# Block copies and additions put out one by one by a count of the DMA queue, in a one-core hybrid layer

## The chip, the cores and the metric

The kernel runs on one core of a Trainium2 chip. The metric is the device time of one execution in microseconds, the median of several runs. All arrays are 32-bit floats; matrix products get near to that precision because each operand is split into a high and a low part and three products of the parts are added.

## The reference

One layer for 512 tokens of width 1024: two branches (a gated delta rule, then a rotary retention) read the same projection; their outputs are gated, mixed and added to the input; an MLP with squared ReLU follows.

```python
xn = rmsnorm(x, n_mix_pre)
proj = xn @ w_in                                  # 1024 x 14352
qa, ka, va, za, beta_logit, a_dt, qb, kb, vb, gb, gate_a, gate_b = _split_cols(proj, IN_SIZES)
...                                               # branch A: conv, silu, l2norm, 8 heads, chunks of 64
oa = chunk_gated_delta_rule(qa, ka, va, beta, g)
oa = rmsnorm(oa, norm_a) * jax.nn.silu(za)
ya = oa.reshape(b, s, A_V) @ w_br_a               # 2048 x 1024
...                                               # branch B: rotary, 4 heads of 256 / 512
ob = chunk_retention(qb, kb, vb)
ob = rmsnorm(ob, norm_b) * jax.nn.silu(gb)
yb = ob.reshape(b, s, B_V) @ w_br_b               # 2048 x 1024
mix = (jax.nn.sigmoid(gate_a) * ya + jax.nn.sigmoid(gate_b) * yb) @ w_out
x = x + rmsnorm(mix, n_mix_post)
hn = rmsnorm(x, n_mlp_pre)
ff = jnp.square(jax.nn.relu(hn @ w_up)) @ w_down  # 1024 x 4096 x 1024
return x + rmsnorm(ff, n_mlp_post)
```

## The kernel before

All weights are read from DRAM in blocks of 512 KB (128 x 4 x 256 or 128 x 2 x 512). `weights` (line 96) issues the load of a block into a `raw` tile on the queue of SyncE (SP). Then ScalarE (ACT) casts it to the high part `whi` (L119) and VectorE (DVE) subtracts to get the low part `wlo` (L120). The raw tiles come from pools of two buffers: `ring`, and from the end of head 0 of branch B on also `ych`, in turn.

There are three stages. *Phase A* (to about 490 us) makes branch A. Its products are issued in an order that a planner, the class `Clock`, writes from costs: `Clock.matmul` (L598), `Clock.transpose` (L607). Four gate chains (`g2` = 0 to 3) end it piece by piece; each makes `og` (an activation on ACT at L1228, a product on DVE at L1230) from what a transpose left, and the next transpose and products need it. *Branch B* goes through four heads h. At the change of a head come the products of the decayed scores with the values (L86 to L88, tiles `dl`), on ACT the squares `osq` of the result (L1419), and the loads of the next head's query and key weights. The products of value and gate projection of a head, and the two output gates ga and gb, go through `token_product` (L247). The *MLP* is last (after about 1000 us).

Nine column pairs of the weights, ga, vg0 to vg3, gb and three of `w_down` (dn0 to dn2), are multiplied by a scheme with seven block products in place of eight (`seven`). It needs four sums of weight blocks. The class `BlockSums` makes them in DRAM, by the DMA engines alone: each `copy` (L138, on SP's queue) copies 512 KB from the weights to a tile `sums`, and each addition (`add_blocks`, L166, on the queue of GpSimd, POOL) adds 512 KB to it, as a DMA that accumulates. An addition waits for its copy and for earlier additions that it reads. There are 9 x 8 = 72 copies and 72 additions. Later, `block_weights` (L153) loads the sums like weights.

How they are placed before the change: from the 14th load on, each call of `weights` is followed by one copy on SP's queue while the list `trickle` is longer than `later_copies` (32, after head 0 16, in the MLP 8 and 0). Additions go out in batches: 14, 14 and 12 at the gate chains g2 = 1, 2 and 3; 8 behind the load of `dec` in heads 2 and 3; 8 in each of two groups of the MLP. POOL's queue, which keeps the order, also carries these loads and stores of branch B: `rope` (the rotary table), `dec` (a head's decay, one buffer), `ya_d` (branch A's output put by in DRAM) and `ya` (the same fetched again).

`tc.issue_after` sets only where an instruction stands in the order of its queue; it makes nothing wait. `high_priority(ahead)` in `split_weights` puts a cast up to 200 places ahead in ACT's and DVE's order.

Of the kernel before, what the change touches and what calls it, by code (L numbers as in the profile page):

```python
# [10 lines left out]
F32 = mybir.dt.float32  # L11
F32R = mybir.dt.float32r
# [3 lines left out]
ALU = mybir.AluOpType  # L16
# [3 lines left out]
P = 128  # L20
T = 512
D = 1024
# [4 lines left out]
OFF_QB, OFF_KB, OFF_VB, OFF_GB = 6160, 7184, 8208, 10256  # L27
OFF_GA, OFF_GBR = 12304, 13328
SMALL_US, CONV_US, TOK_US, PK_US, INV_US, DB_US = 10.5, 6.5, 2.5, 2.0, 46, 1.2
VT_US, KS_US, PX_US, PC_US, GATE_US, FEAT_US, INV_PRIO, CONV_PRIO, SMALL_PRIO, KEY_PRIO, DECAY_US, AHEAD, TR_US, REC_PRIO, OUT_PRIO = 2.5, 2.4, 3.5, 2.4, 11.0, 1.0, 0, 600, 800, 600, 20.0, 700, 2.2, 900, 900  # L30
# [31 lines left out]
def hybrid_block_kernel(ctx: ExitStack, tc: tile.TileContext, a: dict, out: bass.AP):  # L62
    nc = tc.nc
    x_d = a["x"][0]
    w_in = a["w_in"][0]
    w_br = [a["w_br_a"][0], a["w_br_b"][0]]
# [4 lines left out]
    raw_pools = [(ring, "raw")]  # L71
    loads = itertools.count()
    trickle = []
    later_copies = [32]
    ahead = [200]
# [5 lines left out]
    dr = ctx.enter_context(tc.tile_pool(name="dr", bufs=2, space=DRAM))  # L81

    def mm3(ps, lhs, rhs, first, last):
        lh, ll = lhs
        rh, rl = rhs
        nc.tensor.matmul(ps, lh, rh, start=first, stop=False)  # L86
        nc.tensor.matmul(ps, lh, rl, start=False, stop=False)  # L87
        nc.tensor.matmul(ps, ll, rh, start=False, stop=last)  # L88
# [18 lines left out]
    def copy_block(load):  # L107
        sums, part, k = trickle.pop(0)
        with tc.issue_after(load.ins):
            sums.copy(part, k)  # L110

# [14 lines left out]
    class BlockSums:  # L126


        def __init__(self, src, c1, c2, tag):
            def block(kh, c):  # L130
                return src[4 * kh * P : 4 * (kh + 1) * P, c : c + 512].rearrange("(k p) c -> p k c", p=P)

            self.w12, self.first = block(0, c2), [block(0, c1), block(0, c1), block(1, c2), block(1, c1)]
            self.t = [dr.tile([P, 4, 512], F32, tag=f"{tag}{i}", name="sums", bufs=1) for i in range(4)]
            trickle.extend((self, i, k) for i in (2, 1, 3, 0) for k in (0, 2))

# [3 lines left out]
        def adds(self):  # L140

            for i, k in ((2, 0), (1, 0), (3, 0), (2, 2), (1, 2), (3, 2), (0, 0), (0, 2)):
                src = (self.w12, self.t[2], self.w12, self.t[1])[i]
                yield self.t[i][:, k : k + 2, :], src[:, k : k + 2, :]
# [15 lines left out]
    adds = itertools.chain.from_iterable(sums.adds() for sums in [ga_sums] + vg_sums + [gb_sums] + down_sums)  # L160

    def add_blocks(mark, n):

        with tc.issue_after(mark.ins):
            for dst, src in itertools.islice(adds, n):
                tc.keep_in_program_order(nc.gpsimd.dma_start(dst, src, accum_op=ALU.add))  # L166

# [66 lines left out]
    def token_product(quarters):  # L234

        pinned = []

        def product(pss, x, ks, wts, first):
            wh, wl = wts
            xh, xl = quarters[x]  # L240
            for t in range(2):
                tt = slice(t * P, (t + 1) * P)
                for kk in range(2):
                    k = 2 * ks + kk
                    lhs, rhs = (xh[:, k, tt], xl[:, k, tt]), (wh[:, kk, :], wl[:, kk, :])
                    for i in range(3):
                        m = nc.tensor.matmul(  # L247
                            pss[t], lhs[i // 2], rhs[i % 2],
                            start=first and k + i == 0, stop=k + i == 5, skip_group_check=not first,
                        )  # L250
# [415 lines left out]

    clock = Clock()

    def product_features(src, xs, c0, ncols, kts, krow0, finish):
# [176 lines left out]
    ya_marks = []  # L846
# [58 lines left out]
    with delta_rule:  # L905
# [297 lines left out]
        def gate_chain(g2):  # L1203
# [4 lines left out]
            for hh in range(2):  # L1208
                for t in range(4):
# [99 lines left out]
        )  # L1309
        prev = ogs[3]  # L1310
        ahead[0] = 200


    with tc.tile_pool(name="pb", bufs=1) as pb_:
        rope = pb_.tile([P, 2, T], F32, name="rope")
        nc.gpsimd.dma_start(rope, a["c_rope"])
        cos, sin = rope[:, 0, :], rope[:, 1, :]
# [37 lines left out]
        def scores(h, rows):  # L1355
            dec = pb_.tile([P, T], F32, tag="dec", name="dec")
            decay = nc.gpsimd.dma_start(dec, a["c_decay"][h])
# [8 lines left out]
            if h == 0:  # L1366
                ya_marks.append(ya_partial(3, prev))
            scs = []
            for i in range(4):
                t0 = min(i * P, 256)  # L1370
                n = T - t0
# [11 lines left out]
                nc.vector.tensor_tensor(sc[:, :n2], ps[:, n - n2 : n], dec[:, :n2], ALU.mult)  # L1383
                sh, sl = (pb_.tile([P, n2], F32R, tag=f"s{i}{j}", name="s") for j in range(2))
                nc.scalar.copy(sh, sc[:, :n2])
# [57 lines left out]
        for h in range(4):  # L1443
            scs, og = scores(h, rows)
            if h == 0:

                def gate_a(t, half, src):
# [37 lines left out]
        kept = []  # L1485
        for i in (1, 0, 3, 2):
            keep = None
            if i != 2:
                w = pf.tile([P, 2, D], F32R, tag=f"f{i}", name="keep")
                keep = w[:, 0, :], w[:, 1, :]  # L1490
            kept.append(weights(w_br[1], 12 + len(kept), 1, 0, D, keep))
        mix = [act.tile([P, 8, T], F32R, tag="actT", name="actT") for _ in range(2)]
# [24 lines left out]
    with tc.tile_pool(name="pm", bufs=1) as pm:  # L1517
# [112 lines left out]
        wpost = broadcast_row(a["norm_mlp_post"][0], "post")  # L1630
        later_copies[0] = 8

# [101 lines left out]
        for grp in range(4):  # L1734
            sq = Squares(grp)
            for half in range(2):
                for th in (None,) if grp or half else (1, 0):
                    tt = slice(0, T) if th is None else slice(256 * th, 256 * th + 256)
                    pss = feature_major(w_up, [h[:, :, tt] for h in hn], grp * 1024 + half * 512, 512, 8)
                    for f in range(4):  # L1740
                        with tc.high_priority(150 * half):
                            sq.take(half, f, pss[f], th)
                            if half and f % 2 and not sq.last:
                                sq.first_sums(f - 1)
            if grp < 2:
                later_copies[0] = 0
                add_blocks(sq.sums_mark, 8)
            if not sq.last:
# [51 lines left out]
```

## Time and profile before

| | |
|---|---|
| three runs | 1361.91, 1370.55, 1366.67 us; median 1366.67 |
| the profiled execution | 1371.82 us, span 1370.0 us |
| TensorE (PE) | 1338.1 us busy, 98% of the span |
| VectorE (DVE), ScalarE (ACT) | 885.6 us (65%), 634.0 us (46%) |
| GpSimd (POOL) | 97.3 us (7%), nearly all of it issuing DMAs |
| DMA queue q1 (SP's and ACT's transfers) | 185.10 MB, 42.6% of the 16 DMA engines' span |
| DMA queue q0 (POOL's transfers) | 49.45 MB, 20.7% |

The span runs from the first to the last instruction of one execution; the time is what the device reports for it, a little more. The busy share of an engine is a mean over stages; PE's idle time, about 24 us in 1370, lies in a few gaps. Percentages of the queues are the time of their packets against all 16 engines, so a share near 1 in a stretch means that the transfers there are limited by the engines.

### The profile page before, as it was taken

To read this page: it belongs to the slowest core of one execution; us is meant where nothing else is said; L and a number is where in the kernel's file an instruction comes from. 1 tells how busy PE (TensorE), PEld (TensorE's weight loads), DVE (VectorE), ACT (ScalarE), POOL (GpSimd) and SP (SyncE) were. 2 spreads that over 40 slices of the span, in tenths; PEclk is the share of its full clock that TensorE was granted. 3 is DMA by queue.
4 is the path that set the end of the run, shared out by engine and by line. 5 is a ranking of instruction groups with operands and counts; after the bars stand their busy time and mean duration, and the time that the engine had idled before them with its cause. 6 is when DMAs were issued, how large, how long until landed. Compare 5 with 4: busy or idle time off the path is not lost.

```text
span 1370.0 us, 17550 instructions
## 1 busy us (share of the span) xinstructions
PE 1338.1 (98%) x6639; PEld 1106.6 (81%) x6639; DVE 885.6 (65%) x1515; ACT 634.0 (46%) x1118; POOL 97.3 (7%) x110
## 2 busy tenths in 40 slices
PE   9999999989999999999989989999999999999997
PEld 7888888878878878788868878888789888888886
DVE  6889858474466356767457567578776744828535
ACT  5783336543333423553433343355355736436441
POOL 2101110012010000000100100000001111000000
PEclk9999999999999999999999999999999999999999
DMA  5349995799892234693893882465549899635421
GB/s 185 130 139 220 216 179 127 159 231 221 193 223 65 75 116 135 218 305 105 202 287 102 193 212 69 146 212 172 192 139 275 218 284 206 218 98 168 135 82 62
DMA packets 114437, 236.79 MB, mean 173 GB/s; under 512 B 7398, under 2 KB 31120, under 8 KB 113840
## 3 DMA queue, kind: packets, MB, share of 16 engines
q1 hardware_dynamic: 95792, 185.10, 42.6%
q0 software_dynamic: 17824, 49.45, 20.7%
q8 instruction: 52, 0.85, 0.3%
q10 hardware_dynamic: 736, 1.12, 0.2%
q14 instruction: 33, 0.27, 0.1%
HBM read 231.43 MB, written 79.71 MB: 227 GB/s over the span
## 4 chain that ended last, share of the span: by engine, by line
PE 80%; DMA 8%; DVE 6%; ACT 5%; issue 1%; ACTq 0%; DVEq 0%; POOLq 0%
PE mm L598 17%; PE mm L87 10%; PE mm L86 10%; PE mm L88 10%; PE mm L247 10%; PE dl L247 10%; PE dl L598 6%; DMA raw<-in_w_in_dram 5%; DVE wlo L120 2%; DMA raw<-sums 2%; ACT whi L119 1%; PE tr L607 1%; PE tr L327 1%; PE dl L86 1%; PE dl L87 1%
## 5 line engine op out<-in xcount | busy, mean ns | idle before, releaser
L120 DVE TENSOR_TENSOR wlo<-raw,whi 128x1024 fp32r<-128x1024 f32 x254 | 310.0, 1222 | 264.1 <-ACT whi L119 263.4
L119 ACT CAST whi<-raw 128x1024 fp32r<-128x1024 f32 x254 | 266.9, 1052 | 419.8 <-PE mm L87 92.5
L598 PE MATMUL mm<-actT,whi 128*128 128x512 f32 x448 | 146.3, 408 | 0.0
L247 PE MATMUL mm<-whi,xsum 128*128 128x512 f32 x384 | 121.5, 390 | 0.0
L88 PE MATMUL mm<-hn,wlo 128*128 128x512 f32 (+1 forms) x288 | 105.4, 366 | 0.0
L87 PE MATMUL mm<-hn,whi 128*128 128x512 f32 (+1 forms) x288 | 105.3, 366 | 0.0
L86 PE MATMUL mm<-hn,whi 128*128 128x512 f32 (+1 forms) x288 | 105.3, 366 | 0.0
L598 PEld LDWEIGHTS mm<-actT,whi 128*128 128x128 f32 x448 | 81.7, 191 | 15.5
L247 PE MATMUL dl<-whi,actT 128*128 128x512 f32 x288 | 92.2, 390 | 0.0
L598 PE MATMUL mm<-whi,actT 128*128 128x512 f32 x256 | 87.8, 406 | 1.1 <-DVE qf L827 1.0
L598 PE MATMUL mm<-actT,wlo 128*128 128x512 f32 x224 | 88.7, 396 | 0.0
L247 PEld LDWEIGHTS mm<-whi,xsum 128*128 128x128 f32 x384 | 71.9, 188 | 14.9
L247 PE MATMUL mm<-wlo,xsum 128*128 128x512 f32 x192 | 75.0, 391 | 0.1
L598 PE MATMUL mm<-whi,og 128*128 128x512 f32 x192 | 64.2, 402 | 0.0
L247 PEld LDWEIGHTS dl<-whi,actT 128*128 128x128 f32 x288 | 54.1, 188 | 11.1
L86 PEld LDWEIGHTS mm<-hn,whi 128*128 128x128 f32 x288 | 54.3, 189 | 8.8
L88 PEld LDWEIGHTS mm<-hn,wlo 128*128 128x128 f32 x288 | 54.3, 189 | 8.7
L87 PEld LDWEIGHTS mm<-hn,whi 128*128 128x128 f32 x288 | 54.3, 189 | 8.7
L247 PE MATMUL dl<-whi,ffq 128*128 128x512 f32 x192 | 61.0, 389 | 0.0
L166 POOL DMA_DIRECT2D sums<-sums x36 | 30.0, 833 | 387.0 <-DMA sums<-in_w_in_dram 189.7
L598 PEld LDWEIGHTS mm<-whi,actT 128*128 128x128 f32 x256 | 48.1, 188 | 11.4 <-issue 1.7
L247 PE MATMUL dl<-wlo,actT 128*128 128x512 f32 x144 | 56.3, 391 | 0.6 <-DVE wlo L120 0.6
(376 smaller groups left out, 2804.6 us busy)
## 6 DMA issues: line engine op xcount, KB each, us to landing
raw<-in_w_in_dram SPq DMA_DIRECT2D x97, 512.0 KB, 5.0
raw<-sums SPq DMA_DIRECT2D x72, 512.0 KB, 4.5
sums<-in_w_in_dram SPq DMA_DIRECT2D x48, 512.0 KB, 8.8
sums<-sums POOLq DMA_DIRECT2D x36, 512.0 KB, 8.1
raw<-in_w_up_dram SPq DMA_DIRECT2D x36, 512.0 KB, 4.9
raw<-in_w_down_dram SPq DMA_DIRECT2D x26, 512.0 KB, 4.6
sums<-in_w_in_dram POOLq DMA_DIRECT2D x24, 512.0 KB, 11.4
sums<-in_w_down_dram SPq DMA_DIRECT2D x24, 512.0 KB, 10.6
```

The costliest lines, as they stand in the source:

```text
L86: nc.tensor.matmul(ps, lh, rh, start=first, stop=False)
L87: nc.tensor.matmul(ps, lh, rl, start=False, stop=False)
L88: nc.tensor.matmul(ps, ll, rh, start=False, stop=last)
L119: nc.scalar.copy(hi[:, :n], raw[:, :n])
L120: nc.vector.tensor_tensor(lo[:, :n], raw[:, :n], hi[:, :n], ALU.subtract)
L166: tc.keep_in_program_order(nc.gpsimd.dma_start(dst, src, accum_op=ALU.add))
L247: m = nc.tensor.matmul(pss[t], lhs[i // 2], rhs[i % 2], start=first and k + i == 0, stop=k + i == 5, skip_group_check=not first,)
L327: nc.tensor.transpose(ps, src, ident)
L598: m = tc.keep_in_program_order(nc.tensor.matmul(*args, **kwargs))
L607: tc.keep_in_program_order(nc.tensor.transpose(ps, src, ident if by is None else by))
```

## The change

Line numbers move: after the change a weight load is L102, a copy L165, an addition L132, a load of sums L185, `rope` L1345, `dec` L1386, `ya_d` L1486 and `ya` L1501.

*The count.* A function `pace` is called behind every load, those of `block_weights` too. It keeps two times in us: `spent`, how far PE's work is (in phase A the planner's clock, then the sum over matmuls by `tick`), and `queued`, until when the DMA engines are taken by what was issued. Each load adds 2.0, each copy 2.0, each addition 3.4; while less than 6.0 us are queued, the next job goes out behind the load, a copy and an addition in turn. An addition is ready when all copies of its group have been put out. `queued` begins at 60. `BlockSums.weights` would put out what is missing of a group before its loads. Batches and `later_copies` are gone.

*The queue.* `rope`, `dec`, `ya_d` and `ya` are issued by ACT (`nc.scalar`). `dec` has two buffers.

*Space.* The second pool of raw tiles, `ych`, opens before the unit of gate ga, where it was after the end of head 0. The eight score tiles of a head lie in one tile `s` of 2560 columns, and the fourth kept block of `w_br_b` lies there too at the end of the stage, where it was in `ring`.

```diff
+JOBS_FROM, LOAD_US, COPY_US, ADD_US, BACKLOG = 60.0, 2.0, 2.0, 3.4, 6.0
...
+    trickle, later_adds = [], []
+    added, spent, queued, clocks = [False], [None], [JOBS_FROM], []
...
+    def tick(n):
+        if spent[0] is not None:
+            spent[0] += 0.0135 + n / 2400
...
-        if paced and i >= 13 and len(trickle) > later_copies[0]:
-            copy_block(load)
+        pace(load)
...
+    def pace(load):
+
+        if clocks:
+            spent[0] = clocks[0].now
+        if spent[0] is None:
+            return
+        queued[0] = max(queued[0], spent[0]) + LOAD_US
+        with tc.issue_after(load.ins):
+            while (trickle or later_adds) and queued[0] < spent[0] + BACKLOG:
+                ready = len(later_adds) > -(-len(trickle) // 8) * 8
+                if ready and (added[0] or not trickle):
+                    add_block()
+                    queued[0] += ADD_US
+                elif trickle:
+                    copy_block()
+                    queued[0] += COPY_US
+                added[0] = not added[0]
+
+    def add_block():
+        dst, src = later_adds.pop(0)
+        tc.keep_in_program_order(nc.gpsimd.dma_start(dst, src, accum_op=ALU.add))
...
         def weights(self, i, ks):
+            while any(job[0] is self for job in trickle):
+                copy_block()
+            while any(dst is t for dst, src in later_adds for t in self.parts):
+                add_block()
             return block_weights(self.t[i - 1][:, 2 * ks : 2 * ks + 2, :])
...
-        nc.sync.dma_start(raw.rearrange("p (k c) -> p k c", k=2), block)
+        load = nc.sync.dma_start(raw.rearrange("p (k c) -> p k c", k=2), block)
+        pace(load)
...
-            if g2:
-                add_blocks(ya_marks[-1], (0, 14, 14, 12)[g2])
...
+        spent[0] = clocks.pop().now
...
-        nc.gpsimd.dma_start(rope, a["c_rope"])
+        nc.scalar.dma_start(rope, a["c_rope"])
...
-            dec = pb_.tile([P, T], F32, tag="dec", name="dec")
-            decay = nc.gpsimd.dma_start(dec, a["c_decay"][h])
-            if h > 1:
-                add_blocks(decay, 8)
+            dec = pb_.tile([P, T], F32, tag="dec", name="dec", bufs=2)
+            nc.scalar.dma_start(dec, a["c_decay"][h])
...
+            sall = pb_.tile([P, 2560], F32R, tag="s", name="s")
...
+                raw_pools.append((pb_, "ych"))
                 gate_unit(ga_sums, OFF_GA, gate_a)
                 for t in range(4):
-                    nc.gpsimd.dma_start(ya_d[:, t, :], acc_t[:, t, :])
+                    nc.scalar.dma_start(ya_d[:, t, :], acc_t[:, t, :])
...
-            if h == 0:
-                raw_pools.append((pb_, "ych"))
-                later_copies[0] = 16
...
-            kept = nc.gpsimd.dma_start(ya[i], ya_d[:, 2 * i : 2 * i + 2, :])
+            kept = nc.scalar.dma_start(ya[i], ya_d[:, 2 * i : 2 * i + 2, :])
...
-            if grp < 2:
-                later_copies[0] = 0
-                add_blocks(sq.sums_mark, 8)
```

How this moves instructions, at three places. First the queue of SP early in phase A, at about 96 to 121 us of the profile before; `raw` are loads, `sums` copies. Before:

```order
L96 DMA raw<-in_w_in_dram 128x2x512
L138 DMA sums<-in_w_in_dram 128x2x512
L96 DMA raw<-in_w_in_dram 128x2x512
L138 DMA sums<-in_w_in_dram 128x2x512
L96 DMA raw<-in_w_in_dram 128x4x256
L138 DMA sums<-in_w_in_dram 128x2x512
```

and after the change, around the same loads:

```order
L102 DMA raw<-in_w_in_dram 128x2x512 x2
L165 DMA sums<-in_w_in_dram 128x2x512
L102 DMA raw<-in_w_in_dram 128x2x512
L165 DMA sums<-in_w_in_dram 128x2x512 x2
L102 DMA raw<-in_w_in_dram 128x2x512
L165 DMA sums<-in_w_in_dram 128x2x512 x2
L102 DMA raw<-in_w_in_dram 128x4x256
L165 DMA sums<-in_w_in_dram 128x2x512 x2
L102 DMA raw<-in_w_in_dram 128x4x256
L165 DMA sums<-in_w_in_dram 128x2x512 x2
```

Before, copies begin seven loads earlier and go one behind each load; now they begin later, nine of them behind five loads. In the rest of phase A there are about three copies to four loads; before, one to each up to the 56th load and none behind it.

Second, the queue of POOL from the end of phase A to head 3. Before:

```order
L166 DMA sums<-in_w_in_dram 128x2x512 x2
L1316 DMA rope<-in_c_rope_dram 128x1024
L1357 DMA dec<-in_c_decay_dram 128x512 x2
L1455 DMA ya_d<-acc 128x1024 x4
L1357 DMA dec<-in_c_decay_dram 128x512
L166 DMA sums<-in_w_in_dram 128x2x512
L166 DMA sums<-sums 128x1024 x2
L166 DMA sums<-in_w_in_dram 128x2x512
L166 DMA sums<-sums 128x1024 x2
L166 DMA sums<-in_w_in_dram 128x2x512 x2
L1357 DMA dec<-in_c_decay_dram 128x512
L166 DMA sums<-in_w_down_dram 128x2x512
```

and after the change:

```order
L132 DMA sums<-in_w_in_dram 128x2x512 x3
L132 DMA sums<-sums 128x1024 x2
L132 DMA sums<-in_w_in_dram 128x2x512
L132 DMA sums<-sums 128x1024 x2
L132 DMA sums<-in_w_in_dram 128x2x512 x2
L132 DMA sums<-in_w_down_dram 128x2x512
L132 DMA sums<-sums 128x1024 x2
L132 DMA sums<-in_w_down_dram 128x2x512
```

Nothing but additions is left there; no `dec` stands ahead of them.

Third, the queue of SP at the change from head 2 to head 3 (about 790 to 826 us before), loads of query and key weights and of `w_br_b`. Before there is no copy:

```order
L96 DMA raw<-in_w_in_dram 128x4x256 x4
L96 DMA raw<-in_w_br_b_dram 128x2x512 x4
```

and after the change:

```order
L102 DMA raw<-in_w_in_dram 128x4x256
L165 DMA sums<-in_w_down_dram 128x2x512
L102 DMA raw<-in_w_in_dram 128x4x256
L165 DMA sums<-in_w_down_dram 128x2x512
L102 DMA raw<-in_w_in_dram 128x4x256 x2
L165 DMA sums<-in_w_down_dram 128x2x512
L102 DMA raw<-in_w_br_b_dram 128x2x512
L165 DMA sums<-in_w_down_dram 128x2x512
L102 DMA raw<-in_w_br_b_dram 128x2x512
L165 DMA sums<-in_w_down_dram 128x2x512
```

Copies of `w_down` that stood in the MLP now stand at the changes of heads; at the change from head 1 to head 2 there are about as many copies as before. In the MLP none is left.

More of the change, by code (lines that the diff above doesn't have):

```diff
@@ L72, in hybrid_block_kernel @@
     loads = itertools.count()
-    trickle = []
-    later_copies = [32]
+    trickle, later_adds = [], []
+    added, spent, queued, clocks = [False], [None], [JOBS_FROM], []
     ahead = [200]
@@ L85, in mm3 @@
         rh, rl = rhs
+        tick(3 * int(np.prod(rh.shape[1:])))
         nc.tensor.matmul(ps, lh, rh, start=first, stop=False)
@@ L105, in weights, with copy_block @@
             return split_weights(raw, n, nk, keep, ahead[0] if i >= 6 else 0)
-    def copy_block(load):
+    def pace(load):
[17 more added lines that the diff above has]
+        tc.keep_in_program_order(nc.gpsimd.dma_start(dst, src, accum_op=ALU.add))
+    def copy_block():
         sums, part, k = trickle.pop(0)
-        with tc.issue_after(load.ins):
-            sums.copy(part, k)
+        sums.copy(part, k)
     def split_weights(raw, n, nk, keep=None, ahead=200):
@@ L134, in __init__ @@
             self.t = [dr.tile([P, 4, 512], F32, tag=f"{tag}{i}", name="sums", bufs=1) for i in range(4)]
+            self.parts = []
             trickle.extend((self, i, k) for i in (2, 1, 3, 0) for k in (0, 2))
@@ L143, in adds @@
                 src = (self.w12, self.t[2], self.w12, self.t[1])[i]
-                yield self.t[i][:, k : k + 2, :], src[:, k : k + 2, :]
+                self.parts.append(self.t[i][:, k : k + 2, :])
+                yield self.parts[-1], src[:, k : k + 2, :]
         def weights(self, i, ks):
+            while any(job[0] is self for job in trickle):
+                copy_block()
+            while any(dst is t for dst, src in later_adds for t in self.parts):
+                add_block()
             return block_weights(self.t[i - 1][:, 2 * ks : 2 * ks + 2, :])
@@ L159, in hybrid_block_kernel @@
     down_sums = [BlockSums(w_down[grp * D : (grp + 1) * D, :], 0, 512, f"dn{grp}") for grp in range(3)]
[L160 to L166, printed above, removed]
+    for sums in [ga_sums] + vg_sums + [gb_sums] + down_sums:
+        later_adds.extend(sums.adds())
     def quarter(xs, kh, th):
@@ L245, in product @@
                     lhs, rhs = (xh[:, k, tt], xl[:, k, tt]), (wh[:, kk, :], wl[:, kk, :])
+                    tick(1536)
                     for i in range(3):
@@ L667, in hybrid_block_kernel @@
     clock = Clock()
+    clocks.append(clock)
     def product_features(src, xs, c0, ncols, kts, krow0, finish):
@@ L1368, in scores @@
             scs = []
+            sall = pb_.tile([P, 2560], F32R, tag="s", name="s")
+            done = 0
             for i in range(4):
@@ L1383, in scores @@
                 nc.vector.tensor_tensor(sc[:, :n2], ps[:, n - n2 : n], dec[:, :n2], ALU.mult)
-                sh, sl = (pb_.tile([P, n2], F32R, tag=f"s{i}{j}", name="s") for j in range(2))
+                sh, sl = sall[:, done : done + n2], sall[:, done + n2 : done + 2 * n2]
+                done += 2 * n2
                 nc.scalar.copy(sh, sc[:, :n2])
@@ L1486, in hybrid_block_kernel @@
         for i in (1, 0, 3, 2):
-            keep = None
             if i != 2:
                 w = pf.tile([P, 2, D], F32R, tag=f"f{i}", name="keep")
-                keep = w[:, 0, :], w[:, 1, :]
-            kept.append(weights(w_br[1], 12 + len(kept), 1, 0, D, keep))
+            else:
+                w = pb_.tile([P, 2560], F32R, tag="s", name="keep")[:, 0:2048].rearrange("p (a c) -> p a c", a=2)
+            kept.append(weights(w_br[1], 12 + len(kept), 1, 0, D, (w[:, 0, :], w[:, 1, :])))
         mix = [act.tile([P, 8, T], F32R, tag="actT", name="actT") for _ in range(2)]
@@ L1630, in hybrid_block_kernel @@
         wpost = broadcast_row(a["norm_mlp_post"][0], "post")
-        later_copies[0] = 8
         class Squares:
```

## The prediction

> **What bounds the kernel now.** I read the page first, for which engine is the bound, then the waits of that engine, then the timeline around each long wait, then the DMA issues there.
>
> ```profile
> span 1370.0 us, 17550 instructions
> PE 1338.1 (98%) x6639; PEld 1106.6 (81%) x6639; DVE 885.6 (65%) x1515; ACT 634.0 (46%) x1118; POOL 97.3 (7%) x110
> PE dl L86 <- ACT osq L1419: 8.7, 2, 5.1
> PE tr L607 <- DVE og L1230: 7.8, 2, 4.7
> PE mm L598 <- DVE qf L827: 1.0, 1, 1.0
> PE dl L247 <- DVE wlo L120: 0.6, 1, 0.6
> ```
>
> TensorE (PE) is busy for 98%; the change alters no matrix product. So it can only win what PE loses now: idle time, and slow time behind it. Four waits are long (8.7 + 7.8 = 16.5 us together); the rest are near 1 us or less. Here they are in the timeline (start, duration, and in brackets the idle time before), then the stretches after them (length, busy time of PE, PEld, DVE, ACT and POOL, granted clock, DMA share, GB/s).
>
> ```profile
> 306.61 1.11 PE L607 MATMUL tr<-cmat,vt 128*128 128x128 f32 x4 [4.73 <-DVE og L1230]
> 400.33 0.66 PE L607 MATMUL tr<-cmat,vt 128*128 128x128 f32 x4 [3.05 <-DVE og L1230]
> 707.18 0.39 PE L86 MATMUL dl<-vr,s 128*128 128x512 f32 x1
> 707.40 0.39 PE L87 MATMUL dl<-vr,s 128*128 128x512 f32 x1
> 713.13 0.80 PE L86 MATMUL dl<-vr,s 128*128 128x512 f32 x1 [5.11 <-ACT osq L1419]
> 714.15 0.63 PE L88 MATMUL dl<-vr,s 128*128 128x512 f32 x1
> 714.58 0.63 PE L86 MATMUL dl<-vr,s 128*128 128x512 f32 x1
> 814.12 0.50 PE L86 MATMUL dl<-vr,s 128*128 128x512 f32 x1 [3.57 <-ACT osq L1419]
> 306.20:309.60 3.40, 2.99 (x9) 2.57 (x10) 2.51 (x4) 1.21 (x2) 0.00 (x0) 0.50 0.86 132
> 401.80:405.20 3.40, 3.40 (x10) 2.53 (x9) 2.10 (x3) 0.27 (x1) 0.00 (x0) 0.50 1.07 222
> 712.40:719.20 6.80, 6.07 (x14) 4.79 (x15) 2.19 (x4) 1.96 (x7) 0.00 (x0) 0.50 1.01 360
> 814.80:818.20 3.40, 3.40 (x10) 2.63 (x9) 0.10 (x1) 0.83 (x4) 0.00 (x0) 0.50 0.48 153
> ```
>
> Each of the four stalls is followed by 3.4 or 6.8 us at half clock. Matmuls then start 0.43 us apart (714.15 to 714.58) instead of 0.22 to 0.23 (707.18 to 707.40), so a share of 1 - 0.23/0.43 = 0.465 of PE's busy time there is lost: 2.99, 3.40, 6.07 and 3.40 us of busy time give 1.4, 1.6, 2.8 and 1.6 us. With their idle time the stalls cost 6.1, 4.6, 7.9 and 5.2 us, 23.8 in all.
>
> What is late? ScalarE (ACT) casts each loaded weight block (L119) and does the activations that PE waits for, in one fixed order. In the rows below ACT stands before a cast until a load lands, and only then comes to the activation that PE needs. The weights themselves are not needed yet. The rows of the chain give a load's issue and time to landing; two POOL rows, additions and dec at their issue; then follow, for 590 to 613, 684 to 700 and 785 to 804 us, the copies (SPq) and additions (POOLq) issued, with their median landing times, and the landing times of the loads of line 96; the last row is the one load issued at 388.8 us.
>
> ```profile
> 302.93 1.04 ACT L119 CAST whi<-raw 128x1024 fp32r<-128x1024 f32 x1 [4.95 <-DMA raw<-in_w_in_dram]
> 710.40 1.04 ACT L119 CAST whi<-raw 128x1024 fp32r<-128x1024 f32 x1 [1.74 <-DMA raw<-in_w_in_dram]
> 712.41 0.57 ACT L1419 ACTIVATE osq<-dl 128x512 f32<-128x512 f32 x1
> 290.21 12.62 DMA raw<-in_w_in_dram
> 695.64 14.66 DMA raw<-in_w_in_dram
> 798.95 12.35 DMA raw<-in_w_in_dram
> 289.33 1.14 POOL L166 DMA_DIRECT2D sums<-in_w_in_dram  x1 [1.60 <-DMA sums<-in_w_in_dram]
> 649.23 0.55 POOL L1357 DMA_DIRECT2D dec<-in_c_decay_dram  x1 [71.50 <-DVE sc L1383]
> sums<-in_w_in_dram SPq DMA_DIRECT2D x7, 512.0 KB, 7.5
> DMA to landing us min/median/max: 4.2/5.9/8.1
> sums<-in_w_down_dram SPq DMA_DIRECT2D x3, 512.0 KB, 13.0
> sums<-in_w_in_dram POOLq DMA_DIRECT2D x2, 512.0 KB, 13.7
> sums<-sums POOLq DMA_DIRECT2D x1, 512.0 KB, 8.9
> DMA to landing us min/median/max: 5.8/11.4/15.4
> sums<-sums POOLq DMA_DIRECT2D x2, 512.0 KB, 7.9
> sums<-in_w_down_dram POOLq DMA_DIRECT2D x2, 512.0 KB, 13.4
> DMA to landing us min/median/max: 7.2/11.2/12.4
> DMA to landing us min/median/max: 8.4/8.4/8.4
> ```
>
> The three stretches are the same place (the change of a retention head) in three heads. In the first there are seven copies and no addition: no load takes over 8.1 us and PE does not stall. In the second there are three copies and three additions, in the third four additions and no copy, and loads take up to 15.4 and 12.4 us. So additions that meet the boundary's loads make the stalls; copies alone do not. The second and third batch are there because they stand on POOL's queue behind dec, which waited 71.5 us for its only buffer.
>
> **The change part by part.** *Amount of traffic.* It is the same: 72 copies, 72 additions, the same loads.
>
> ```profile
> q1 hardware_dynamic: 95792, 185.10, 42.6%
> q0 software_dynamic: 17824, 49.45, 20.7%
> 300.00:400.00 100.00, 14.68 (x15) 0.98 0.92 214
> 400.00:500.00 100.00, 0.25 (x1) 0.98 0.33 88
> ```
>
> Queue q1 takes 0.426 x 1370 = 584 us of all engines for 185.1 MB, or 1.65 us for each 512 KB (353 of them); q0 0.207 x 1370 = 284 us for 49.45 MB, or 3.0 us (94). The count in the change holds 2.0 for a load or a copy and 3.4 for an addition, 13 to 21% above these, and lets a job out while less than 6 us stand in it. By these prices a load that is issued finds about 6 us ahead of it and lands some 8 us later, unless additions held back by their copies come together. The last two rows are POOL's issues of additions for 100 us each: 15 and 1 now.
>
> *The stall at 708 us.* PE could run on at 708.02, so the load of 695.64 would have to land 5.1 us sooner, in 9.5 us instead of 14.66. By the order, some three copies and one addition stand beside the loads there instead of three copies and three additions: 2 x 3.0 = 6 us of traffic less, which would give 14.66 - 6 = 8.7 us, and near the stretch at 590, whose worst is 8.1. Gain 7.9 (bounds 0 and 7.9).
>
> *The stall at 810.* The load of 798.95 may take 12.35 - 3.57 = 8.8 us. Four additions (12 us) become three copies and one or two additions (5 + 4.5 = 9.5 us), spread evenly. I take 5.2 (bounds 0 and 5.2); this is the tighter one.
>
> *The stall at 397.* Its load (issued at 388.8, landing at 397.2) must be 3.05 us sooner; one addition stands before it instead of three, 6 us less. Gain 4.6 (0 to 4.6).
>
> *The stall at 302.* Here the same two additions stay and one copy goes, 1.65 us directly, some more through the load before it. I leave 2 us of 4.73 and no half clock, since the wait of 1.0 us (for qf) in the first fence was followed by none and that of 3.05 by one: gain 2.7 + 1.4 = 4.1 (0 to 6.1). The Trainium skill ("TensorE: Matmul & The Clock Gate", "Part 1: The HAM clock gate") says that a whole idle window of about 3.4 us halves the clock, with windows that run freely. This trace agrees in length (3.4 and 6.8 us at 0.50), but 3.05 us of idleness sufficed; by either, a remainder of 2 us keeps the clock.
>
> *Four raw buffers during the ga unit.* The wait of 0.6 us for wlo goes: 0.6 (0 to 0.6).
>
> *Nine copies behind five loads at 96 to 121 us,* where five were: 4 x 1.65 = 6.6 us of traffic more. Loads are about 6 us apart there, so most fits. Cost 1.5 (0 to 6.6).
>
> *rope, dec, ya_d and ya on ACT's queue.* There they wait for DVE or PE results that ACT's next activations need too; behind them stand casts. No such wait is in this trace on ACT; POOL's waits for the same data (up to 71.5 for dec) ended on a buffer that now is double, and nothing below the 0.57 us of one activation can be read off for the rest. I take 0.5 (0 to 5.1, a boundary's stall again). The Trainium skill ("DMA: Bandwidth & Descriptors", "Issuing engines are not separate DMA queues") says that transfers from different engines share the 16 DMA engines, so another queue buys no bandwidth. By that rule alone this part brings nothing. The rows agree: the sharing is what delays loads, and what the move brings is order, additions no longer standing behind dec.
>
> Sum: 7.9 + 5.2 + 4.6 + 4.1 + 0.6 - 1.5 - 0.5 = 20.4 us. The profiled execution took 1371.8 us (span 1370.0), so 1351.4. It was 5.15 us above the median of 1366.67; were that a constant offset, the median would be 1346.3. The stalls were read off the slower execution, so I stay nearer the first: **1350.0 us**. All stalls gone at no cost would be 1371.8 - 24.4 = 1347.4, less the offset 1342.3.
>
> **The rivals.**
>
> *A: only the two stalls at the heads go.* For it: in phase A (to 490 us) copies are thinned only from one to about 0.75 per load, and additions still follow their copies at once, so they can meet any load; the two at 302 are unmoved. Against: 397 loses two of three. Gain 7.9 + 5.2 + 0.6 - 2.0 = 11.7: 1360.1, with the same 1.4 off 1358.7.
>
> *B: the stalls move.* The change doesn't do what it says: the count decides an instruction's place, but an addition starts when its copies have landed and POOL is free, and nothing ties it to a load. Each stretch keeps as many pairs of additions, and of 24 us at most a third is won: 8 - 2 = 6, about 1365. For it: POOL's waits are for copies, none for a load. Against: 590 to 613 shows that what counts is how many meet a boundary, and the batch behind dec is gone for sure.
>
> *C: slower.* The count is kept full from 96 to beyond 840 us, so jobs stand in front of every load, where between 400 and 600 us there was one addition. If a load in front of a boundary then regularly lands later than 9.5 us after its issue, the four head changes cost 7.9 each and the four gate chains of phase A 6.1 each: 31.6 + 24.4 against 23.8 now, 1404; with half of them, 1387. For it: 284 us of additions at 3.0, twice a copy's price, now go beside the loads of heads that had none. Against: the count's prices lie above the measured ones, so it should drain, and seven copies at 590 did no harm.
>
> **How the numbers follow.** My forecast 0.55, A 0.23, B 0.10, C 0.12. The forecast's own range is 1342 to 1355; A and B reach to 1366, C beyond. Leaving C and the ends out gives 1343 to 1366 as the range. Single runs spread from 1361.91 to 1370.55, so about 1% (13.7 us) can be told from no change: faster is below 1353.0. Of the forecast 0.50 lies there, and 0.05 of A; within 1% lie 0.05 + 0.18 + 0.10 = 0.33; slower is C with 0.12.
>
> **What would show it.** In the changed profile PE's waits for osq and for og should fall from 16.5 us to under 4, no stretch at 0.50 should stand near 708, 810 and 397, loads at the head changes should land within 9 us, and POOL's additions should have some 8 to 12 in each 100 us to 900. Stalls at og alone would be A; new stalls of 3 to 5 us elsewhere behind late casts B, and eight of them C. An ACT row of rope, ya_d or ya with microseconds of idle time before the next cast would make the 0.5 wrong; stalls for qf or wlo at 100 to 125 us the 1.5.

## The result: 1.3% faster, and the profile after

Four runs of the changed kernel took 1347.26, 1352.33, 1345.96 and 1349.07 us, median 1348.16. The kernel before stood at 1367.22 (four runs). The ratio is 0.9868, 95% interval 0.9827 to 0.9908. The forecast was 1350.0. The profiled execution took 1347.26 us with a span of 1345.1, where the sum had put 1351.4.

The page of the changed kernel, then the longest waits of its PE (a wait of 1.2 us at the start, the same before, is left out):

```profile
span 1345.1 us, 17540 instructions
PE 1327.4 (99%) x6639; PEld 1101.2 (82%) x6639; DVE 884.8 (66%) x1515; ACT 634.4 (47%) x1118; POOL 90.9 (7%) x99
PE tr L636 <- DVE og L1258: 1.5, 2, 1.2
PE dl L93 <- DVE wlo L146: 1.4, 1, 1.4
PE dl L627 <- DVE rn L1021: 1.0, 1, 1.0
PE mm L627 <- DVE qf L857: 1.0, 1, 1.0
```

The number of matrix products is the same. PE is busy 10.7 us less, mostly because nothing runs at half clock behind the four stalls any more (7.4 us by the prediction's count); the rest of the 24.9 us of span is idle time, which falls from 31.9 us (1370.0 - 1338.1; the 24 named with the profile before are too few) to 17.7. `osq` is gone from the list, `og` fell from 7.8 to 1.5 us. New are 1.4 us for `wlo` (near 510 us, 0.5 before) and 1.0 for `rn` (near 144). The transfers moved to ACT stand on a queue of their own, q10 (1.12 MB before, 6.89 now), and not on q1, where the table before puts ACT's transfers.

At the head changes the loads (line 102) land sooner. For 575 to 597, 669 to 690 and 767 to 790 us, the copies and additions issued, and the landing times of the loads:

```profile
sums<-in_w_down_dram SPq DMA_DIRECT2D x3, 512.0 KB, 6.4
sums<-sums POOLq DMA_DIRECT2D x1, 512.0 KB, 8.5
DMA to landing us min/median/max: 4.5/5.3/8.3
sums<-in_w_down_dram SPq DMA_DIRECT2D x3, 512.0 KB, 6.6
sums<-in_w_down_dram POOLq DMA_DIRECT2D x1, 512.0 KB, 11.1
DMA to landing us min/median/max: 5.5/5.7/8.3
sums<-in_w_down_dram SPq DMA_DIRECT2D x5, 512.0 KB, 6.7
sums<-sums POOLq DMA_DIRECT2D x1, 512.0 KB, 9.7
DMA to landing us min/median/max: 5.2/5.5/10.0
```

One addition in each, three to five copies, and 8.3 to 10.0 us at worst (the prediction gave 9), against 15.4 and 12.4 before. The additions are spread out, though not as evenly as the 8 to 12 in each 100 us that the prediction named: POOL's issues in 300 to 400, 400 to 500 and 800 to 900 us are now

```profile
300.00:400.00 100.00, 9.89 (x10) 1.00 0.81 189
400.00:500.00 100.00, 11.60 (x12) 1.00 0.82 197
800.00:900.00 100.00, 0.85 (x1) 1.00 0.60 169
```

(POOL's busy time, the number of additions, the granted clock, the DMA share and GB/s.)

### The profile page after: what moved, and what is told of

Same layout as the page of the kernel before. It is cut to its first block, busy times and chain, and to the rows that moved or that the text cites. A ratio compares the mean times of both kernels' runs of the same rounds, so it can differ in the third digit from the quotient of the medians.

```text
span 1345.1 us, 17540 instructions
## 1 busy us (share of the span) xinstructions
PE 1327.4 (99%) x6639; PEld 1101.2 (82%) x6639; DVE 884.8 (66%) x1515; ACT 634.4 (47%) x1118; POOL 90.9 (7%) x99
## 3 DMA queue, kind: packets, MB, share of 16 engines
q10 hardware_dynamic: 2320, 6.89, 1.4%
## 4 chain that ended last, share of the span: by engine, by line
PE 86%; DVE 6%; ACT 4%; DMA 3%; issue 1%; DVEq 0%; ACTq 0%
PE mm L627 16%; PE mm L276 13%; PE dl L276 12%; PE mm L92 11%; PE mm L93 11%; PE mm L94 11%; PE dl L627 6%; DMA raw<-in_w_in_dram 2%; DVE wlo L146 1%; PE tr L356 1%; PE dl L93 1%; PE dl L94 1%; PE dl L92 1%; PE tr L636 1%; PE mm L591 1%
## 5 line engine op out<-in xcount | busy, mean ns | idle before, releaser
L132 POOL DMA_DIRECT2D sums<-sums x36 | 29.9, 830 | 443.2 <-DMA sums<-in_w_in_dram 238.7
```

## The experiments

The theory: additions that meet the loads of a head change or of a gate chain delay a cast on ACT, and behind it the activation that PE waits for. Rivals: the copies delay the loads; the count alone, or the queue alone, does the work.

**No additions.** Edit to the kernel before:

```diff
-            for dst, src in itertools.islice(adds, n):
+            for dst, src in itertools.islice(adds, 0):
```

> The kernel before without the 72 additions (the sums hold only their first block); all copies, loads, casts and products stay. If additions beside loads make the four stalls, all four go with their half clock: 22 to 24 us faster than before, near 1344, and loads at the head changes land within 9 us. If the copies behind every load make them, at least the two stalls of phase A stay, where a copy follows each load, and the gain is 13 us or less.

Median 1346.50 (ratio 0.9833, 0.9784 to 0.9883), 22.0 us under 1368.45, the median of before in that series. All four stalls are gone, with every copy still in its place; PE's longest waits there:

```profile
PE mm L598 <- DVE qf L827: 1.0, 1, 1.0
PE dl L247 <- ACT whi L119: 0.9, 1, 0.9
PE dl L247 <- DVE wlo L120: 0.8, 1, 0.8
```

So it was the additions, not the copies. The change comes within 2 us of a kernel that makes no additions at all. That is no strict floor: the waits of 0.9 and 0.8 us stand together near 550 us, at the ga unit with its two raw buffers, and 3.4 us at half clock follow them.

**Additions without accumulation.**

```diff
-                tc.keep_in_program_order(nc.gpsimd.dma_start(dst, src, accum_op=ALU.add))
+                tc.keep_in_program_order(nc.gpsimd.dma_start(dst, src))
```

> The kernel before with additions that only overwrite (POOL issues the same 72 transfers without accumulation; the sums are wrong by that). If an addition burdens the engines because it accumulates, queue q0 takes some 1.7 us of all engines for 512 KB in place of 3.0, and the four stalls shrink or go: 1348 to 1360. If a second queue beside SP's is what delays the loads, price and stalls stay: 1366 to 1372.

One run: 1345.88 us, span 1344.1. The order and the batches are those of before and POOL still waits as long for `dec`, yet no stall is left. The third row is q0 in the run without additions:

```profile
q1 hardware_dynamic: 95792, 185.10, 43.5%
q0 software_dynamic: 13216, 49.45, 12.1%
q0 software_dynamic: 2848, 11.70, 2.5%
POOL dec L1357 <- DVE sc L1383: 169.9, 3, 71.5
PE mm L598 <- DVE qf L827: 1.0, 1, 1.0
```

The same 49.45 MB on q0 take 12.1% instead of 20.7%: 0.121 x 1344 / 94 = 1.73 us of all engines for 512 KB instead of 3.0. Both are means over q0's 94 blocks, of which only 72 are additions. The other 11.70 MB take 0.025 x 1346 = 34 us in the run without additions; with these taken off, an addition costs (284 - 34) / 72 = 3.5 us, and one that only overwrites (163 - 34) / 72 = 1.8 us. It is the accumulation that is dear, not a second queue. And `dec` waits 71.5 us as ever, so that wait does harm only through what stands behind it.

**The queue's part alone.** The kernel before with `rope`, `dec` (two buffers), `ya_d` and `ya` on ACT's queue; copies and batches as before.

```diff
-            dec = pb_.tile([P, T], F32, tag="dec", name="dec")
-            decay = nc.gpsimd.dma_start(dec, a["c_decay"][h])
+            dec = pb_.tile([P, T], F32, tag="dec", name="dec", bufs=2)
+            decay = nc.scalar.dma_start(dec, a["c_decay"][h])
```

> The kernel before, with only rope, dec (two buffers), ya_d and ya moved to ACT's queue; count and order of copies as before, batches kept. If the two stalls at the head changes (708 and 810 us, 13.1 us with their half clock) come from additions held behind dec, they go or fall below 2 us, while the stalls at og (302 and 397 us, 10.7 us) stay: about 12 us faster than before. If the count of the queue is what removes all four, all four stay and the time is that of before within 3 us. If additions merely move to the next boundary, a new stall for osq of 3 to 5 us stands near 600 us.

1353.61 us (0.9888, 0.9846 to 0.9930): 14.8 us gained. No wait for `osq` above 0.6 us is left, and no new one stands near 600. The stalls at `og` stay, smaller than in the first profile (see below).

**A second buffer for dec, and nothing else.**

```diff
-            dec = pb_.tile([P, T], F32, tag="dec", name="dec")
+            dec = pb_.tile([P, T], F32, tag="dec", name="dec", bufs=2)
```

> The kernel before with a second buffer for dec and nothing else; rope, dec, ya_d and ya stay on POOL's queue. If the long wait of dec for its only buffer (71.5 us) is what put the additions beside the loads at 690 and 795 us, the two stalls for osq go and the time is that of the queue's part alone, about 1354. If standing behind ya_d and ya on that queue is enough, one of them stays, 1360 to 1365.

1353.69 us (0.9891, 0.9850 to 0.9933), 16.4 under the 1370.07 of before there: as much as the whole move to ACT's queue. The timeline of POOL tells why; first the kernel before, then this one:

```profile
649.77 1.24 POOL L166 DMA_DIRECT2D sums<-in_w_in_dram  x1
658.30 0.87 POOL L166 DMA_DIRECT2D sums<-sums  x1 [7.29 <-DMA sums<-in_w_in_dram]
...
692.15 2.63 POOL L166 DMA_DIRECT2D sums<-in_w_in_dram  x2
```

```profile
598.64 1.20 POOL L166 DMA_DIRECT2D sums<-in_w_in_dram  x1 [25.01 <-DMA sums<-in_w_in_dram]
608.64 0.87 POOL L166 DMA_DIRECT2D sums<-sums  x1 [8.80 <-DMA sums<-in_w_in_dram]
...
640.71 2.63 POOL L166 DMA_DIRECT2D sums<-in_w_in_dram  x2
645.07 0.61 POOL L1357 DMA_DIRECT2D dec<-in_c_decay_dram  x1 [1.74 <-DVE sc L1383]
```

A batch of eight takes 42 us, since its additions wait for each other. Released by `dec` at 649, the middle of a head, it ends at 692, on the loads of the next head change. With the second buffer it starts as soon as its copies have landed, at 599, and ends at 641, where no load is pressing. Not the number of additions in a head changed, but their phase.

**The count alone.** The changed kernel with the four transfers back on POOL's queue and one buffer of `dec`.

```diff
-        nc.scalar.dma_start(rope, a["c_rope"])
+        nc.gpsimd.dma_start(rope, a["c_rope"])
...
-            dec = pb_.tile([P, T], F32, tag="dec", name="dec", bufs=2)
-            nc.scalar.dma_start(dec, a["c_decay"][h])
+            dec = pb_.tile([P, T], F32, tag="dec", name="dec")
+            nc.gpsimd.dma_start(dec, a["c_decay"][h])
```

> The changed kernel with rope, dec (one buffer), ya_d and ya back on POOL's queue. The count then sets phase A: the stalls at og near 302 and 397 us stay away (10 us gained on the kernel before). Additions stand behind dec again for up to 70 us and come out in a row when it is released, so I expect one or two stalls for osq of 3 to 5 us with half clock, 5 to 13 us over the changed kernel: 1353 to 1361. If the count alone does the work and the queue is nothing, it equals the changed kernel within 2 us. If the held additions become late for the loads of their sums, it is slower than before.

1372.12 us, ratio 1.0017 (0.9991 to 1.0043): no gain at all, where 1353 to 1361 had been expected, 7 to 15 us under the 1368.45 of before. The mechanism was as expected, its size was not. The stalls at `og` are gone, two for `osq` are there, and waits for `rn`, `wlo` and `whi` besides:

```profile
PE dl L92 <- ACT osq L1449: 9.2, 2, 5.7
PE mm L276 <- DVE wlo L146: 3.1, 5, 0.8
PE dl L627 <- DVE rn L1021: 2.0, 1, 2.0
POOL rope L1345 <- PE tr L636: 123.4, 1, 123.4
POOL dec L1386 <- DVE sc L1412: 100.9, 2, 64.2
sums<-sums POOLq DMA_DIRECT2D x2, 512.0 KB, 9.6
DMA to landing us min/median/max: 11.3/12.9/17.2
```

The last two rows are 585 to 611 us, a head change that had no addition before. In the count's order additions stand behind `rope`, which waits 123 us for the end of phase A; they follow late and meet those loads, which take 11.3 to 17.2 us. A part of the loss is not POOL's queue: early in phase A, where instructions and their order are those of the changed kernel, PE waited 1.99 us for `rn` at 144 (1.05 there) and then ran 10.2 us at half clock, so that the transpose of the gate chain near 302 began at 307.98 instead of 303.34.

**The count, with two buffers of dec, on POOL's queue.** As the last, but `bufs=2` kept.

> The changed kernel with rope, dec, ya_d and ya back on POOL's queue, but dec keeps its two buffers. If the one buffer of dec is what undid the count there, the stall for osq at 811 us goes; additions still stand behind rope and ya_d on that queue (rope waited 123 us there), so the one at 608 us may stay: 1350 to 1360. If rope and ya_d do as much harm as dec, both stay and the time is near that of before, 1365 to 1373.

1358.56 us (0.9951, 0.9929 to 0.9973). The stall for `osq` near 811 us is gone, the one at 604 is still there (4.2 us), behind `rope` (122.4 us of waiting). Its ratio lies above the interval of the whole change: with the count, the queue that carries the four transfers matters as well as the buffer. All four were moved together; that it is `rope` is read from the trace, not tested by itself.

**The whole change beside the queue's part alone,** both once more.

> The changed kernel once more, beside the one with the queue's part alone. If the count is worth what the profiles show (the stalls at og near 302 and 397 us, 1.70 and 2.10 us with 3.4 us of half clock there, and 0.77 us for wlo), it is 4 to 6 us faster than that one: about 1348 against 1353.

> The kernel before with only rope, dec, ya_d and ya on ACT's queue, once more. 14 to 16 us faster than before, 4 to 6 slower than the whole change. If the 4 to 6 us between them were chance of single executions, both medians lie within 2 us.

1348.08 us (0.9858, 0.9824 to 0.9892) and 1351.18 (0.9864, 0.9829 to 0.9900). The medians differ by 3.1 us here and by 5.4 with the first series, in the direction expected, but single runs overlap (1345.99 to 1355.49 against 1345.87 to 1353.01) and so do the intervals of the ratios. The times alone do not show that the count brings something on top of the queue. The profiles do: PE's longest wait for `og` is 2.1 to 4.7 us in the four that have the accumulating additions and not the count, and 0.5 to 1.2 us in seven of the eight that have it (2.8 in the eighth, the earlier start below). How much time that is stays open.

**The count's size.**

```diff
-JOBS_FROM, LOAD_US, COPY_US, ADD_US, BACKLOG = 60.0, 2.0, 2.0, 3.4, 6.0
+JOBS_FROM, LOAD_US, COPY_US, ADD_US, BACKLOG = 60.0, 2.0, 2.0, 3.4, 24.0
```

> The changed kernel with 24 us in place of 6 us let into the queue: jobs go out much earlier and several behind one load. If the size of the count is what keeps loads on time, loads land 10 us and more after their issue, casts come late and stalls of 3 to 5 us with half clock return at og and at osq: 8 to 25 us slower than the changed kernel. If additions only follow their copies and the order of the queue matters little, the time stays within 3 us of the changed kernel.

With 24 us 1354.90 (0.9890, 0.9842 to 0.9939), 6.7 us over the change's 1348.16: just under the range given. The stall is at another place than named, in the recurrence of phase A, and so is the late load: a row of the chain (issue and time to landing), then PE's longest wait. The profiled execution was the slowest of the four.

```profile
452.49 18.92 DMA raw<-in_w_in_dram
PE dl L627 <- ACT vt L1208: 4.2, 1, 4.2
```

> The changed kernel with 4 us in place of 6 let into the queue: fewer jobs beside each load, one copy at most behind a load at 100 to 125 us, part of the additions of w_down later, up to the MLP. If shorter queues help further, the rests of the changed kernel (1.2 us at og near 302, 1.4 for wlo at 510, 1.05 for rn at 144) shrink and it is 1 to 3 us faster. If the floor is reached (the kernel without additions took 1346.5), it is the same within 2 us. If jobs put off meet the MLP's loads, a stall stands after 1000 us.

With 4 us in place of 6, 1356.54 (0.9912, 0.9881 to 0.9943): 8.5 us slower than the change beside it. The phase A rests did go (no wait for `rn` and none over 0.6 us for `og`), but additions put off came up in the MLP: a load of sums issued at 1066.48 took 13.06 us, and PE stood 3.15 us at 1077.6, followed by 3.4 us at half clock. This stall and its half clock are some 4.7 of the 7.1 us between the two profiled spans; the rest was not taken apart. So 6 lies between two values that both cost. It is again the place that counts: the kernel before had 16 additions in the MLP and no wait over 0.6 us there.

**An earlier start of the count** (`JOBS_FROM` 40 for 60).

> The changed kernel with the count beginning at 40 in place of 60: copies begin four loads earlier, and the pairs behind one load lie before 110 us. If the nine copies behind five loads are what makes the load of 126.5 us take 13.6 us and PE wait 1.0 us for rn at 144, that wait goes and nothing comes for it: 1 us faster, which only the profile can show. If the first 100 us cannot take copies (waits of small vectors there), new waits of 1 us or more stand between 60 and 110 us.

The wait for `rn` is gone (the two loads from 120.7 us on took 10.3 us at most instead of 13.6) and none took its place before 110 us; so the crowd of nine copies is what cost that 1.0 us and, it seems, the 10.2 us at half clock in the profile of the count alone. The time, 1348.74 (0.9886, 0.9847 to 0.9925), cannot be told from the change: in the profiled execution PE stood 2.75 us for `og` at 390 instead.

**The raw pool opened late.**

```diff
-                raw_pools.append((pb_, "ych"))
                 gate_unit(ga_sums, OFF_GA, gate_a)
...
+            if h == 0:
+                raw_pools.append((pb_, "ych"))
             rows = outputs(h, scs)
```

> The changed kernel with the second pool of raw tiles opened after head 0, as before the change. If it is what took away the wait for wlo at 562 us, a wait of 0.5 to 0.8 us for it stands there again. If the additions had made that wait, it stays away.

One run, 1357.60. The wait is back and larger: PE stands 1.33 us for `whi` and 0.75 for `wlo` at 560 to 563, and then runs at half clock for 3.4 us. There is more half clock at 147 (10.2 us) and 516, before this edit changes any instruction; one run does not give a price beyond 2.1 + 1.6 us at this place.

## Why the prediction was right, and what in it was not

*The two head stalls (7.9 and 5.2).* Both went whole, for the reason given: additions held back by `dec`. The kernels without additions, without accumulation and with a second buffer all remove them, each by another step of the chain. Together they were sized 13.1 us; the second buffer alone brought 16.4 in the medians (9 to 21 by its interval).

*The stalls at og (4.1 and 4.6).* In the changed kernel 1.18 us are left at 302, without half clock (2 were expected), and 0.30 at 399. At 397 the way is the one given: POOL issues one addition from 380 to 400 us, where it issued four. At 302 two additions stay, as forecast, and the load that the chain runs through takes 7.2 us instead of 12.6. But the sizes came from one execution. Three other profiles have the very same instructions in the same order up to there and show other waits:

```profile
303.02 0.66 PE L607 MATMUL tr<-cmat,vt 128*128 128x128 f32 x4 [1.70 <-DVE og L1230]
394.44 0.66 PE L607 MATMUL tr<-cmat,vt 128*128 128x128 f32 x4 [2.10 <-DVE og L1230]
303.90 0.69 PE L607 MATMUL tr<-cmat,vt 128*128 128x128 f32 x4 [2.81 <-DVE og L1230]
396.12 0.66 PE L607 MATMUL tr<-cmat,vt 128*128 128x128 f32 x4 [1.34 <-DVE og L1230]
305.98 0.66 PE L607 MATMUL tr<-cmat,vt 128*128 128x128 f32 x4 [3.48 <-DVE og L1230]
397.81 0.66 PE L607 MATMUL tr<-cmat,vt 128*128 128x128 f32 x4 [0.96 <-DVE og L1230]
```

These are the queue's part alone, twice, and the second buffer alone: 1.70 to 3.48 and 0.96 to 2.10 us, where the profile before had 4.73 and 3.05. A transfer lands some microseconds sooner or later from one execution to the next: the load that the wait at 302 hangs on took 9.63, 10.74 and 11.43 us in these three and 12.62 in the profile before. That mis-sized the term: between the queue's part and the whole change the medians leave 3 to 5 us for the count (1 to 3 by the ratios), where 4.1 + 4.6 + 0.6 - 1.5 = 7.8 were put.

*The median against the profiled execution.* 1350.0 was chosen nearer to 1351.4 than to 1346.3. Measured were 1348.16, between them. The stalls of the execution profiled before were probably larger than typical, by its time and by the waits above, so the gain in medians (19.1 us) is smaller than in the two profiles (24.6). That the forecast comes within 2 us of the measured median is in part luck: the head part brought more than its 13.1, the count less than its 7.8, and no row gives the place between 1346.3 and 1351.4.

*The price of an addition (3.0 us against 1.65 for a copy).* Right in kind, too low in size: 3.0 is a mean over all of q0's transfers, and an addition alone costs 3.5 (1.8 without accumulation). So the 3.4 of the count is not 13% above the measured price but at it; only the 2.0 for a load or a copy has room.

*The small terms.* The crowd of copies cost 1.0 us in the profiled execution (1.5 put, for `rn` instead of `qf` or `wlo`), but not in each: among five profiles with the same instructions there, the wait for `rn` was 0.99 to 1.99 us, and in two (the count alone, the late pool) 10.2 us at half clock followed, which put the gate chain near 302 off by 4.6 and 3.5 us. The four raw buffers saved more than 0.6: without them the changed kernel loses 2.1 us and a half-clock stretch there (one run). None of the four transfers on ACT's queue shows a wait there, for which 0.5 was put. What was lost lies elsewhere, and no term foresaw it. In the changed kernel `rope` goes out at 489.61 and lands late, and DVE, which needs it, comes late to the `wlo` of 510:

```profile
489.61 8.96 DMA rope<-in_c_rope_dram
498.67 0.69 DVE L1374 TENSOR_TENSOR ro<-mm,rope 128x512 f32<-128x512 f32 x1 [5.88 <-DMA rope<-in_c_rope_dram]
```

This is the 1.4 us for `wlo`. In all fourteen profiles it goes with that wait of DVE: PE waits 1.4 us in the five where DVE waits 5.5 us or more for `rope` (the whole change twice, with 4 us, with 24 us, and with the late pool), 0.5 in the kernel before (4.5), and not at all in the eight where DVE waits 4.1 or less. With the count or with ACT's queue alone `rope` lands in 5.3 to 6.7 us, with both in 8.5 to 10.7, but for the earlier start (5.5).

*The rivals.* The changed kernel is none of them, but A (only the head stalls go) is nearly what the second buffer or the queue gives by itself, 1353.7 and 1351 to 1354 against the 1358.7 given, since the stalls that stay are smaller. B's new stalls near 600 did not come in the changed kernel. The rule of the Trainium skill that another issuing queue buys no bandwidth ("DMA: Bandwidth & Descriptors", "Issuing engines are not separate DMA queues") agrees: without the count, a buffer reaches the gain of the move (1353.69 against 1353.61). C's mechanism (a queue kept too full delays loads) exists: at 6 us of backlog it shows in the load behind the nine copies (13.6 us) and in `rope`, at 24 it costs 6.7 us. Its large prices were not seen. Its 1387 for half of the stalls does not follow from its own figures: half of 31.6 + 24.4 is 28.0 against 23.8 now, so about 1376.

## What to carry to other kernels

Before tuning how much background traffic goes where, look for what holds it back: an instruction ahead on the same in-order queue that waits for its only buffer can move a whole batch onto the most pressing loads, and a second buffer may be worth more than a new scheduler. Work on one side only can be worth nothing: spreading additions by a count brought no gain while they still stood behind `rope` and `dec`. And read stalls of a few microseconds that hang on DMA landings from several executions before they become terms of a sum.

## What the runs showed of the hardware

*A PE that idles about half of one 3.4 us stretch can lose its clock.* The transitions of the granted clock lie on a grid of 3.4 us: in the kernel before, half clock begins at 306.2, 401.8, 712.4 and 814.8 us, 28, 91 and 30 steps of 3.413 us apart. Windows on that grid, with PE's busy time second and the granted clock third from the end; the first from the kernel before, the next three from the queue's part alone, then one each from the change and the kernel without additions, the last two from the late pool:

```profile
398.40:401.80 3.40, 1.47 (x9) 1.30 (x10) 2.58 (x4) 2.32 (x4) 1.15 (x1) 1.00 0.92 171
299.90:303.30 3.40, 1.70 (x10) 1.12 (x9) 2.88 (x4) 2.17 (x4) 0.85 (x1) 1.00 0.94 311
392.10:395.50 3.40, 1.30 (x9) 0.98 (x8) 2.61 (x4) 2.41 (x5) 1.28 (x2) 1.00 0.93 154
395.50:398.90 3.40, 3.40 (x10) 2.62 (x9) 2.16 (x3) 0.32 (x1) 0.00 (x0) 0.50 1.06 216
510.30:513.70 3.40, 1.96 (x9) 1.52 (x9) 3.40 (x5) 1.05 (x2) 0.00 (x0) 1.00 0.21 63
548.30:551.70 3.40, 1.73 (x7) 0.92 (x6) 1.45 (x2) 1.99 (x2) 0.00 (x0) 1.00 0.30 114
560.20:563.60 3.40, 1.31 (x5) 0.83 (x5) 2.01 (x3) 2.66 (x4) 0.00 (x0) 1.00 0.09 34
563.60:567.00 3.40, 3.40 (x10) 2.65 (x9) 2.75 (x4) 1.47 (x3) 0.00 (x0) 0.50 0.79 183
```

Idle for 2.1 us of the window (busy 1.30 and 1.31) or 1.9 (busy 1.47) the next window is at 0.50; idle for 1.4 (busy 1.96) the clock stays. The edge is not sharp: 1.70 us kept it in the queue's part, 1.67 lost it without additions. On the grids of the fourteen profiles, between 60 and 1335 us, all 17 windows with 1.79 us of idleness or more were followed by half clock, two of the four between 1.60 and 1.74, and below that only two, both near 144 us among 32x32 matmuls (1.15 us in the late pool, 1.41 in the count alone); why is open. Two short waits in one window add up, as at 560 (1.33 and 0.75), and a wait across two windows is shared out: of the 3.05 us at 397, 1.1 lay in a window that half clock did not follow, and 1.9 in the next, which it did. The Trainium skill ("TensorE: Matmul & The Clock Gate", "Part 1: The HAM clock gate") asks for an idle window of about 3.4 us; here little more than half of one was enough, on the free-running grid that it describes. So the prediction's "a remainder of 2 us keeps the clock" does not hold in general: it does only where the grid divides the wait. What saved the term is that 1.18 us were left.

*An accumulating DMA from DRAM to DRAM takes 3.5 us of all 16 engines for 512 KB, an overwriting one 1.8* (both on POOL's queue in this kernel, with q0's other transfers taken off as above; with them in the mean, 3.0 and 1.73).
